# Low parts of the up-projection's weights: a subtraction on VectorE, or a negation on ScalarE and an accumulating DMA

## The chip, the cores and the metric

The kernel runs on one core of a Trainium2 chip. A core has TensorE (matmuls, in the profile PE, its weight loads PEld), VectorE (DVE), ScalarE (ACT), GpSimd (POOL) and SyncE (SP), which issues DMAs. Each engine takes its instructions in the order of its own list and waits at each for the semaphores that it names. The metric is device time in microseconds of one execution.

## What is computed

The reference is one step of a model with two layers of width 1024, over 512 prompt tokens and 8 sequences of 4 new tokens. The 544 tokens are handled together. Layer 0 mixes by gated linear attention (GLA), layer 1 by dilated attention; behind each stands a feed-forward stage. The change lies in that stage only:

```python
def _conv_ffn(h, w_up, conv_w, conv_b, w_down, buf):
    T = h.shape[1]
    u = h @ w_up                                   # 1024 -> 2 x 2816
    ux = jnp.concatenate([buf.astype(u.dtype), u], axis=1)
    c = conv_b + sum(ux[:, i:i + T] * conv_w[i] for i in range(CONV_WIDTH))
    gate, val = jnp.split(c, 2, axis=-1)
    return (jax.nn.silu(gate) * val) @ w_down, ux[:, -(CONV_WIDTH - 1):]
```

Everything is float32.

## The kernel before

Products of float32 accuracy are made of three matmuls. Weights and activations are each split into a high part, the value rounded to 12 bits by a cast to float32r, and a low part, the exact rest. `product` (line 95) multiplies high by high, high weights by low activations and low weights by high activations, for each of the 128-row pieces k of the contraction, into one PSUM tile per half of the tokens. For the up-projection there are 8 pieces and 2 halves (256 and 288 columns), so 48 matmuls in a product; for the down-projection 11 pieces, so 66.

`split_w` (line 85) makes the parts of a weight tile: ScalarE casts to `whi` (line 90), VectorE subtracts that from the raw weights to `wlo` (line 91). `whi` and `wlo` have two buffers each. Raw weights lie in two buffers of the tag `wraw` that all stages share, filled by `load_w` (line 80) through SyncE's queue, whose order is that of the program.

`ffn(l, ...)` runs once for each layer. Its 22 up tiles of 256 columns (128 of the gate, 128 of the value, so two products each) come in two halves of 11. Behind each half stand 8 products of the down-projection, with weights `wd` of 704 KB. A tile's product leaves PSUM on VectorE times 1/rms of the token (line 566), goes through the convolution (lines 576 to 578), silu (129) and the gating (583 to 585), and is split again (588, 589). The row of 1/rms (`rstd`) is worked out from the sums of squares `acc` where it is first asked for: two matmuls `pss` (line 180), two logarithms (181) and an exponential. The activations' parts `xh` and `xl` (157, 158) and the squares (166, 170) are made by `Normed.add` as the stage before finishes each x. In layer 0 the stage also works out tables for the attention: products `pbt` (619) and copies `sk` in DRAM, issued between the weights' loads.

The engines' lists are made when the program is built, by a scheduler that plays the program through on a timeline of its own. Loads on SyncE keep the program's order; the rest is put where that timeline has it ready first. So each place at which the order differs is looked up in the built programs.

Of the kernel before, what the change touches and what calls it, by code (L numbers as in the profile page):

```python
# [12 lines left out]
F32R = mybir.dt.float32r  # L13
# [6 lines left out]
P = 128  # L20
# [16 lines left out]
def trunk(ctx: ExitStack, tc: tile.TileContext, A, O, stage=4):  # L37
# [7 lines left out]
    def dma(out, in_):  # L45
        """Loads, in the order in which they are used."""
        tc.keep_in_program_order(nc.sync.dma_start(out, in_))
# [14 lines left out]
    # ---------------------------------------------------------------- background work  # L62
# [3 lines left out]
    def tick():  # L66
        """One stage of each lane's first generator, between the matmuls of a product."""
        for lane in reversed(lanes):
            if lane:
                try:  # L70
                    next(lane[0])
                except StopIteration:
                    lane.popleft()
# [5 lines left out]
    # ---------------------------------------------------------------- weights  # L79
# [5 lines left out]
    def split_w(raw, k0, k1, c0, m=P):  # L85
        """Two parts of a weight tile that add up to it exactly, each of 12 bits."""
# [10 lines left out]
    def product(w, xh, xl, ranges, done, m=P):  # L97
        """w.T x of float32 accuracy, in two halves of the tokens; done(half, psum) takes each."""
# [12 lines left out]
    # ---------------------------------------------------------------- constants  # L111
# [11 lines left out]
    def exp(out, in_, **kw):  # L123
        last_exp[0] = act(out, in_, AF.Exp, **kw)  # L124

    def silu(out, in_):
        """Behind every Exp so far, as the two sit in different sets of tables."""
# [4 lines left out]
    def log_exp():  # L132
        """The set of tables that holds both, loaded behind the last Silu and ahead of the block."""
# [10 lines left out]
    class Normed:  # L144
        """x * gain in two exact parts, tile by tile as x comes; the row of 1/rms, on every partition,
        is worked out where it is first asked for."""
# [5 lines left out]
        def add(self, k, x, spare=None):  # L152
            """A spare pool: GpSimd takes half of the squares, with a sum of its own."""
# [31 lines left out]
    def scaled(nx, out, scale=None, m=P):  # L185
        """What takes a product: times 1/rms, to SBUF."""
# [12 lines left out]
    # ---------------------------------------------------------------- GLA  # L199
    def gla(nxt):  # L200
# [24 lines left out]
        # the gates' second product: [hi | lo | hi] of the first against [hi | hi | lo] of the weights  # L225
# [21 lines left out]
        # zero outside of what the heads write  # L247
# [9 lines left out]
        def gates(h, G):  # L257
            # log-sigmoid of the gates, before the division
# [12 lines left out]
            # sums of the gates inside of a chunk  # L271
# [22 lines left out]
        def chain(h, q, k, v, G):  # L294
# [3 lines left out]
            # values, token-major  # L298
# [8 lines left out]
            # [hi | lo | hi] of the sample group's values and [hi | hi | lo] of its keys  # L307
# [7 lines left out]
            # decays over whole chunks: F[..., 0:2], [2:5], [5:9] bring keys to the end of chunk 1, 2, 3,  # L315
            # [9:13] queries to the start of the 128 tokens, 13 the state over all of them
# [16 lines left out]
            # the sample group's rows: 32 (b mod 4) + 4 (b // 4) + s  # L333
# [28 lines left out]
            # scores inside of the chunks  # L362
# [23 lines left out]
            # scores against the earlier chunks of the 128 tokens  # L386
# [49 lines left out]
            # sample group  # L436
# [47 lines left out]
        # the output's operands take the places of tiles that the heads are done with  # L484
# [47 lines left out]
    # ---------------------------------------------------------------- ConvFFN  # L532
    def ffn(l, x, nx, dst, tables=None, nxt=None):
        first = load_w(A["wu"][l, 0], KT, 256, "wu")
        with ExitStack() as es:
# [13 lines left out]
            half = NFF // 2  # L549
            for hf in range(2):  # L550
                gh, gl = [], []
                for ii in range(half):
                    next(bt, None)
                    i = hf * half + ii
                    raw = load_w(A["wu"][l, i], KT, 256, "wu") if i else first
                    cc = []
                    for s in range(2):
# [13 lines left out]
                        product(split_w(raw, 0, KT, s * P), nx.xh, nx.xl, BYTOK, done)  # L571
# [30 lines left out]
    # ---------------------------------------------------------------- dilated attention  # L602
    def bias_tables(bp, out):
        """Bias by distance for every group and head, skewed in DRAM so that a strided read gives the
        tile [query, head, key]; distances outside of the window hold NEG."""
        n = (383, 255, 63)
        # the row pitch as read, and the rows as written (number of runs, their pitch, a run's rows, their
        # pitch): each row so much further on as its queries are later
# [29 lines left out]
    def dilated(nx, xold, tables, nxt):  # L638
        first = load_w(A["wdi"][0], KT, 256, "wdi")
        with ExitStack() as es:  # L640
# [33 lines left out]
            # The prompt's tokens by their remainders of the group's dilation. The tiles of groups 1 and 2 take  # L674
            # every fourth token, and their queries lie by the remainder of 16 first.
# [42 lines left out]
            # ---- prompt  # L718
            # a unit: four tiles of 128 queries by 128 keys, or half of that many blocks by two; of a tile
            # its number, its first block of keys, its column and its width. Group 2's tiles are 4 by 32  # L720
            # queries of 4 by 32 keys, of which a query sees its own 32.
# [3 lines left out]
            def split_scores(q, k):  # L725
                """For each of two heads [hi; lo] of its queries, [hi; hi] of its keys, and the keys' lo: two
                products that add up to all but lo by lo."""
# [13 lines left out]
            def softmax(st, h, todo):  # L741
                """exp(scores + bias - max) of tiles of queries, with the max and the sum of it."""
# [586 lines left out]
```

## Time and profile before

| | |
|---|---|
| median of 3 runs | 1809.33 us (1807.87 to 1809.41) |
| the profiled execution, first to last instruction | 1809.7 us |
| TensorE busy | 1792.2 us (99%) |
| VectorE busy | 1091.2 us (60%) |
| ScalarE busy | 804.6 us (44%) |
| GpSimd busy | 224.4 us (12%) |
| DMA, mean over the span | 131 GB/s, 236.24 MB |

Layer 0's feed-forward stage runs from about 278 to 688 us, layer 1's from 1406 us to the end; GLA stands ahead of the first, dilated attention between the two. The profile holds, for one execution, each instruction with its engine, line, duration and what its engine waited for ahead of it. An idle engine matters only where the chain of waits that ends last passes through it.

### The profile page before, as it was taken

The numbers are of one execution on the slowest core, as the hardware profiler recorded it, in microseconds if no ns is written. First come the engines' busy times: TensorE is split into PE (matmuls) and PEld (weight loads), VectorE is DVE, ScalarE is ACT, GpSimd is POOL, SyncE is SP. The second block draws the span as 40 slices with busy tenths as digits, with TensorE's granted clock in tenths as the row PEclk, the third lists the DMA queues.
The fourth block names the chain that finished last, engine by engine and source line by source line (L and its number), as shares of the span: only waits on it lengthen the run. The fifth ranks groups of instructions, "written<-read, shape, count | busy, mean of one in ns | idle before, by whom it ended". The sixth has DMA issues, their size and how long they took to land.

```text
span 1809.7 us, 35651 instructions
## 1 busy us (share of the span) xinstructions
PE 1792.2 (99%) x14774; PEld 1683.1 (93%) x14774; DVE 1091.2 (60%) x2552; ACT 804.6 (44%) x1549; POOL 224.4 (12%) x416
## 2 busy tenths in 40 slices
PE   7999999999999999999999999999999999999999
PEld 7999999999999999988898888888887999999999
DVE  7565556764476645666575656565664667446652
ACT  5454534442244334644556365546452544224431
POOL 3000100110011010111012010201121011001110
PEclk9999999999999999999999999999999999999999
DMA  5033432432422344255436453544474222232232
GB/s 180 27 129 141 151 113 79 151 104 81 149 80 91 102 157 159 83 195 194 170 118 218 174 179 130 205 166 160 155 241 154 71 94 80 81 110 90 75 102 86
DMA packets 55266, 236.24 MB, mean 131 GB/s; under 512 B 11470, under 2 KB 20896, under 8 KB 37056
## 3 DMA queue, kind: packets, MB, share of 16 engines
q1 hardware_dynamic: 36816, 145.61, 23.3%
q0 software_dynamic: 18288, 88.36, 14.0%
q8 instruction: 116, 1.90, 0.4%
q14 instruction: 46, 0.38, 0.1%
HBM read 210.32 MB, written 29.33 MB: 132 GB/s over the span
## 4 chain that ended last, share of the span: by engine, by line
PE 98%; DMA 1%; DVE 1%; issue 0%; ACT 0%; SPq 0%; DVEq 0%; ACTq 0%
PE ps L104 82%; PE po L902 2%; PE pdo L1004 2%; PE pd L944 2%; PE ptr L887 1%; PE psc L795 1%; PE pn L694 1%; PE psc L794 1%; DMA vc<-in_dv 1%; PE pn L695 1%; PE px L391 1%; PE pvt L762 1%; PE psc L797 0%; PE pu L403 0%; PE po L418 0%
## 5 line engine op out<-in xcount | busy, mean ns | idle before, releaser
L104 PE MATMUL ps<-xh,whi 128*128 128x256 f32 (+2 forms) x3056 | 892.0, 293 | 7.1 <-ACT xh L157 5.5
L104 PE MATMUL ps<-xl,whi 128*128 128x256 f32 (+2 forms) x3056 | 886.5, 290 | 3.3 <-DVE xl L158 3.2
L104 PE MATMUL ps<-xh,wlo 128*128 128x256 f32 (+2 forms) x3056 | 886.9, 291 | 0.0
L104 PEld LDWEIGHTS ps<-xh,whi 128*128 128x128 f32 (+1 forms) x3056 | 577.2, 189 | 38.7 <-issue 29.6
L104 PEld LDWEIGHTS ps<-xh,wlo 128*128 128x128 f32 (+1 forms) x3056 | 576.9, 189 | 11.5 <-issue 9.5
L104 PEld LDWEIGHTS ps<-xl,whi 128*128 128x128 f32 (+1 forms) x3056 | 577.2, 189 | 11.1 <-DVE xl L158 5.5
L104 PE MATMUL ps<-gl,whi 128*128 128x272 f32 x704 | 198.8, 287 | 0.0
L104 PE MATMUL ps<-gh,whi 128*128 128x272 f32 x704 | 198.5, 288 | 0.3 <-DVE x L196 0.3
L104 PE MATMUL ps<-gh,wlo 128*128 128x272 f32 x704 | 195.8, 287 | 0.0
L566 DVE TENSOR_TENSOR u<-ps,rstd 128x256 f32<-128x256 f32 x176 | 74.4, 423 | 140.6 <-PE ps L104 140.2
L90 ACT CAST whi<-wu 128x1024 fp32r<-128x1024 f32 x88 | 92.7, 1053 | 97.2 <-PE ps L104 97.2
L104 PEld LDWEIGHTS ps<-gh,whi 128*128 128x128 f32 x704 | 132.2, 188 | 0.5 <-DVE x L196 0.5
L104 PEld LDWEIGHTS ps<-gl,whi 128*128 128x128 f32 x704 | 132.6, 188 | 0.0
L196 DVE TENSOR_TENSOR x<-ps,x 128x272 f32<-128x272 f32 x108 | 46.8, 440 | 141.4 <-PE ps L104 137.7
L104 PEld LDWEIGHTS ps<-gh,wlo 128*128 128x128 f32 x704 | 130.9, 188 | 0.0
L90 ACT CAST whi<-wd 128x768 fp32r<-128x768 f32 x64 | 50.2, 785 | 171.4 <-PE ps L104 142.0
L91 DVE TENSOR_TENSOR wlo<-wu,whi 128x1024 fp32r<-128x1024 f32 x88 | 107.5, 1222 | 30.7 <-ACT whi L90 30.7
L90 ACT CAST whi<-wdi 128x1024 fp32r<-128x1024 f32 x72 | 75.5, 1048 | 79.6 <-PE ps L104 71.1
L91 DVE TENSOR_TENSOR wlo<-wdi,whi 128x1024 fp32r<-128x1024 f32 x72 | 88.0, 1222 | 27.5 <-ACT whi L90 27.1
L572 POOL COPY uo<-u 128x18 f32<-128x18 f32 x88 | 52.3, 594 | 399.6 <-DVE u L568 399.6
L588 ACT CAST gh<-g 128x544 fp32r<-128x544 f32 x44 | 28.5, 648 | 132.6 <-DVE g L585 132.6
L124 ACT ACTIVATE ex<-ex,nm 128x128 f32<-128x128 f32 (+2 forms) x192 | 74.7, 393 | 19.4 <-DVE nm L748 19.1
(307 smaller groups left out, 2409.6 us busy)
## 6 DMA issues: line engine op xcount, KB each, us to landing
wu<-in_wu SPq DMA_DIRECT2D x44, 1024.0 KB, 4.9
wdi<-in_wdi SPq DMA_DIRECT2D x36, 1024.0 KB, 4.8
vc<-in_dv POOLq DMA_DIRECT2D x28, 1024.0 KB, 6.0
wd<-in_wd SPq DMA_DIRECT2D x32, 704.0 KB, 4.2
kc<-in_dkA POOLq DMA_DIRECT2D x16, 1024.0 KB, 5.3
kc<-in_dkB POOLq DMA_DIRECT2D x16, 768.0 KB, 4.8
out_vo<-v POOLq DMA_DIRECT2D x24, 256.0 KB, 3.1
out_ko<-k POOLq DMA_DIRECT2D x24, 256.0 KB, 3.2
```

The lines of the kernel that those rows point to most:

```text
L90: nc.scalar.copy(hi, r)
L91: tt(out=lo, in0=r, in1=hi.bitcast(F32), op=ALU.subtract)
L104: mm(ps[:m, :b - a], ww, xx[k][:, a:b], start=(k == 0 and s == 0), stop=(k == kt - 1 and s == 2))
L124: last_exp[0] = act(out, in_, AF.Exp, **kw)
L196: tt(out=out[:, c], in0=ps, in1=old[:, c], op=ALU.add)
L391: mm(ps[:32 * c, t, 32 * c - 32:32 * c], keys, qh[:, t * P + 32 * c:t * P + 32 * c + 32], start=True, stop=True)
L566: tt(out=u[:, 2 + c0:258 + c0], in0=ps[:, :256], in1=nx.rstd[:, c0:c0 + 256], op=ALU.mult)
L572: nc.gpsimd.tensor_copy(out=uo[:, f, :].rearrange("p (b t) -> p b t", t=2), in_=u[:, 512:566].rearrange("p (b t) -> p b t", t=6)[:, :, :2])
L588: nc.scalar.copy(h_, g)
L902: mm(o, R[g][2][:, kb, r], PT[n - 2][:, h, c:c + P], start=(n == 2 and i == 0), stop=(n - 1 == len(units)), skip_group_check=True)
L944: mm(pd[32 * qd:32 * qd + 32, a0:a1], qz[g][:, qd // 2, qd % 2, 32 * b:32 * b + 32], kc[4 * part + b][:, qd, a0:a1], start=False, stop=(b ...
L1004: mm(po[32 * qd:32 * qd + 32, :], PT[:, t, 32 * qd:32 * qd + 32], vc[t][:, qd, :], start=False, stop=(t == 6), skip_group_check=True)
```

## The change

In `ffn` the up-projection's weights are no longer split by `split_w`. A new function `prepare` loads a raw tile, has ScalarE write its negative, rounded to float32r, for all 256 columns into a new tile `ulo`, and has GpSimd issue a DMA that reads the same weights from DRAM once more and adds them to `ulo`. What is left there is weights minus rounded weights. `parts` makes the high part on ScalarE as before, a product at a time. `prepare` is called one tile ahead, and the stage's first load stands behind those of `cw` and `cs`, no longer ahead of them. The down-projection still uses `split_w`.

```diff
     def ffn(l, x, nx, dst, tables=None, nxt=None):
-        first = load_w(A["wu"][l, 0], KT, 256, "wu")
         with ExitStack() as es:
...
             half = NFF // 2
+
+            def prepare(i):
+                raw = load_w(A["wu"][l, i], KT, 256, "wu")
+                lo = ft.tile([P, KT, 256], F32R, name="ulo", bufs=3)
+                nc.scalar.activation(lo, raw, AF.Copy, scale=-1.0)
+                nc.gpsimd.dma_start(lo.rearrange("p k n -> p (k n)"), A["wu"][l, i], accum_op=ALU.add)
+                return raw, lo
+
+            def parts(raw, lo, c0):
+                hi = wp.tile([P, KT, P], F32R, name="whi", tag="whi")
+                nc.scalar.copy(hi, raw[:, :, c0:c0 + P])
+                return [(hi[:, k, :], lo[:, k, c0:c0 + P]) for k in range(KT)]
+
+            ready = [prepare(0)]
             for hf in range(2):
                 gh, gl = [], []
                 for ii in range(half):
                     next(bt, None)
                     i = hf * half + ii
-                    raw = load_w(A["wu"][l, i], KT, 256, "wu") if i else first
+                    raw, lo = ready.pop()
+                    if i + 1 < NFF:
+                        ready.append(prepare(i + 1))
...
-                        product(split_w(raw, 0, KT, s * P), nx.xh, nx.xl, BYTOK, done)
+                        product(parts(raw, lo, s * P), nx.xh, nx.xl, BYTOK, done)
```

`ulo` has three buffers, in the stage's own pool. That pool takes the memory of the stage ahead: in layer 0 the first `ulo` lies over a tile `ogh` that GLA's output projection reads to its end. In the changed program lines behind the new functions have higher numbers: the negation is line 555, the accumulating DMA 556, the cast of `parts` 561.

The built programs differ at three places. The first is ScalarE's list where layer 0's feed-forward stage begins. `xh` and `sq` belong to the last x of the stage ahead. Before:

```order
L157 ACTIVATE xh_3097<-x,gains 128x544
L166 ACTIVATE sq<-x 128x544
L90 CAST whi<-wu 128x1024
L157 ACTIVATE xh_3162<-x,gains 128x544
L166 ACTIVATE sq<-x 128x544
L181 ACTIVATE rstd<-pss,eps 128x272
L90 CAST whi<-wu 128x1024
L181 ACTIVATE rstd<-pss,eps 128x272
L124 ACTIVATE rstd<-rstd 128x544
```

And the same place in the changed program:

```order
L166 ACTIVATE sq<-x 128x544
L181 ACTIVATE rstd<-pss,eps 128x272 x2
L555 ACTIVATE ulo<-wu 128x2048
L561 CAST whi<-wu 128x1024
L124 ACTIVATE rstd<-rstd 128x544
L561 CAST whi<-wu 128x1024
```

The two casts of the first up tile stood among the last norms; now the negation stands behind both logarithms, and the casts behind it. In layer 1 the negation stands behind the last `sq`, the two casts follow it, and the logarithms follow them.

The second is TensorE's list at the same place, from the last matmul of GLA's output projection. Before, the first up product follows at once, and `pss` comes 52 rows later:

```order
L104 MATMUL ps<-ogh,wlo 128x272
L104 MATMUL ps<-xh_2702,whi 128x256
L104 MATMUL ps<-xl_2703,whi 128x256
L104 MATMUL ps<-xh_2702,wlo 128x256
L104 MATMUL ps<-xh_2766,whi 128x256
```

In the changed program:

```order
L104 MATMUL ps<-ogh,wlo 128x272
L180 MATMUL pss<-acc,ones 128x272 x2
L636 MATMUL pbt<-oh_3198,rb 16x383
L636 MATMUL pbt<-oh_3199,rb 16x255
L636 MATMUL pbt<-oh_3200,rb 16x63
L104 MATMUL ps<-xh_2702,whi 128x256
L104 MATMUL ps<-xl_2703,whi 128x256
L104 MATMUL ps<-xh_2702,whi 128x288
L104 MATMUL ps<-xl_2703,whi 128x288
L104 MATMUL ps<-xh_2702,whi 128x256
L104 MATMUL ps<-xl_2703,whi 128x256
L104 MATMUL ps<-xh_2702,ulo 128x256
```

`pss` and `pbt` moved ahead of all up matmuls, and six matmuls with high parts stand ahead of the first that reads `ulo`. In layer 1 `pss` stands ahead of the up matmuls too.

The third is the turn from the first down half to the second up half, here ScalarE's list in layer 0. Before:

```order
L90 CAST whi<-wd 128x768
L90 CAST whi<-wd 128x640
L90 CAST whi<-wu 128x1024 x3
L576 ACTIVATE c_5442<-u_3187,cw 128x560
```

And in the changed program:

```order
L90 CAST whi<-wd 128x768
L90 CAST whi<-wd 128x640
L555 ACTIVATE ulo<-wu 128x2048
L561 CAST whi<-wu 128x1024 x3
L593 ACTIVATE c_5437<-u_3185,cw 128x560
```

The casts of the twelfth up tile stand behind the negation of the thirteenth. On SyncE's list 12 loads of `wu` stand ahead of the first 8 loads of `wd`, not 11. The twelfth tile keeps one buffer of `wraw` until its casts, behind that down half; in the built program all eight of those loads go to the other buffer, where before they took turns.

## The prediction

> **What bounds the kernel now.** I read the page's busy times first, then the chain of waits, then both halves of the first feed-forward stage by windows.
>
> ```profile
> span 1809.7 us, 35651 instructions
> PE 1792.2 (99%) x14774; PEld 1683.1 (93%) x14774; DVE 1091.2 (60%) x2552; ACT 804.6 (44%) x1549; POOL 224.4 (12%) x416
> ```
>
> TensorE is busy for all but 17.5 us. The chain of waits from 410 to 500 us is a single piece, the matmuls of line 104, and the windows say the same of the up half (277.56 to 421) and of the down half (421 to 488). In a window's row the columns are the length, then busy us and instructions of PE, PEld, DVE, ACT and POOL, then the granted clock, the DMA engines' busy share and GB/s.
>
> ```profile
> 409.93 90.10 PE ps L104 x720
> 277.56:421.00 143.44, 143.44 (x1136) 142.34 (x1135) 96.15 (x171) 61.60 (x78) 22.32 (x44) 1.00 0.33 108
> 421.00:488.00 67.00, 67.00 (x539) 66.83 (x538) 23.84 (x38) 13.97 (x17) 0.20 (x1) 1.00 0.37 127
> ```
>
> One matmul takes 90.10 / 720 = 0.125 us. So one up tile (2 products of 48 matmuls) takes 12.0 us, half of a tile 6.0 and one product of the down half (66) 8.25. TensorE has no idle time in either half. Whatever VectorE is spared there is worth nothing; the change can only add waits, or leave the time as it is.
>
> **What is removed and added in the steady run.** Groups of instructions, with busy us and mean ns, and the DMA table, with KB and us to landing:
>
> ```profile
> L91 DVE TENSOR_TENSOR wlo<-wu,whi 128x1024 fp32r<-128x1024 f32 x88 | 107.5, 1222 | 30.7 <-ACT whi L90 30.7
> L90 ACT CAST whi<-wu 128x1024 fp32r<-128x1024 f32 x88 | 92.7, 1053 | 97.2 <-PE ps L104 97.2
> L90 ACT CAST whi<-wd 128x768 fp32r<-128x768 f32 x32 | 26.8, 839 | 132.7 <-PE ps L104 109.5 <-issue 22.4 <-ACT acc L166 0.8
> L157 ACT ACTIVATE xh<-x,gains 128x544 fp32r<-128x544 f32 x32 | 23.0, 744 | 1.8 <-PE ps L104 0.9 <-DMA x<-in_xT 0.5 <-DVE x L196 0.3
> L588 ACT CAST gh<-g 128x544 fp32r<-128x544 f32 x44 | 28.5, 648 | 132.6 <-DVE g L585 132.6
> wu<-in_wu SPq DMA_DIRECT2D x44, 1024.0 KB, 4.9
> vc<-in_dv POOLq DMA_DIRECT2D x28, 1024.0 KB, 6.0
> wd<-in_wd SPq DMA_DIRECT2D x32, 704.0 KB, 4.2
> ```
>
> VectorE loses 88 subtractions, 107.5 us, all of it beside matmuls: 0. ScalarE gains 44 negations of 2048 columns. From 768 to 1024 columns a cast grows by 214 ns, so 2048 columns take 1.05 + 4 x 0.214 = 1.91 us, and a form with a scale takes 0.10 more (744 against 648): 2.0 us, 88 us in all. Beside 12.0 us of matmuls per tile this is hidden too. GpSimd issues 44 DMAs that carry another 46 MB. It has nothing queued there but copies of 18 columns, so its queue costs nothing.
>
> The trace has no accumulating DMA. Call its time from issue to landing X. The nearest row is a plain load of the same size from GpSimd's queue, 6.0 us, which is the lower bound: the same bytes must move. A store of 8 KB shows the part that doesn't scale:
>
> ```profile
> scr<-st POOLq DMA_DIRECT2D x8, 8.0 KB, 2.3
> ```
>
> So 3.7 us of the 6.0 is moving. An accumulation reads its destination as well as its source, so I take the moving part twice, X = 2.3 + 2 x 3.7 = 9.7 us. Three passes, 13.4, are the upper end. Nothing suggests less than a plain load.
>
> The Trainium skill ("Collectives: The Full Stack", on the fold count and why AG, RS and AR differ) says that an add inside the DMA costs through its second source read, not through the add, and gives 62.28 against 32.35 GB/s. By that ratio X would be 9.4 and the whole sum 0.6 us less; no run here shows it yet.
>
> In the steady run a negation stands ahead of the next tile's cast on ScalarE. The load that it waits for goes out when the tile before last has been cast (1.05 us into a tile), lands 4.9 later, the negation takes 2.0 and the cast 1.05: 9.0 us, where the cast is needed at 12.0. That leaves 3.0 us. The accumulation then has about 16 us until its low parts are used. With X = 9.7 I put this at 0.
>
> **The first start, near 278 us.** Here the change moves instructions. The rows show the end of the output projection as it runs now:
>
> ```profile
> 255.87 0.33 SPq L47 DMA_DIRECT2D wu<-in_wu  x1
> 277.56 0.28 PE L104 MATMUL ps<-xh,whi 128*128 128x256 f32 x1
> 277.63 1.05 ACT L90 CAST whi<-wu 128x1024 fp32r<-128x1024 f32 x1 [3.78 <-PE ps L104]
> 277.76 0.44 DVE L196 TENSOR_TENSOR x<-ps,x 128x272 f32<-128x272 f32 x1 [2.16 <-PE ps L104]
> 279.24 0.64 ACT L166 ACTIVATE sq<-x 128x544 f32<-128x544 f32 x1
> 279.86 0.78 DVE L158 SCALAR_TENSOR_TENSOR xl<-x,gains,xh 128x544 fp32r<-128x544 f32 x1
> 280.56 0.72 DVE L170 TENSOR_TENSOR acc<-acc,sq 128x544 f32<-128x544 f32 x1
> 284.71 0.49 ACT L181 ACTIVATE rstd<-pss,eps 128x272 f32<-128x272 f32 x1 [4.82 <-PE pss L180]
> ```
>
> From the chain of waits, pss and the products of the tables (pbt), which run between the up matmuls now:
>
> ```profile
> 284.21 0.92 PE pss L180 x4
> ...
> 287.51 1.28 PE pbt L619 x6
> ```
>
> Now the first up product starts at 277.56, the moment the projection ends, and the sum of squares (pss) is slipped in 6.6 us later. In the changed order pss stands ahead of every up matmul, and the first negation stands on ScalarE behind both logarithms of pss. Step by step: the last x is complete at 277.76 + 0.44 = 278.2; xh takes 0.74 to 278.9; xl 0.78 and acc 0.72 follow on VectorE, to 280.4; pss starts there, its first logarithm 0.5 later, and with two of 0.49 ScalarE is free at 282.0. The negation ends at 284.0. Only then can GpSimd issue the accumulation, which lands at 284.0 + X. Meanwhile TensorE can do pss (0.92), pbt (1.28) and the 6 high-part matmuls that stand ahead of the first low one (0.75), 2.95 us. The stage's first load, moved behind those of cw and cs on SyncE, goes out at 255.87 now and isn't wanted before 282.0: 0. The start is late by 284.0 + 9.7 - 277.56 - 2.95 = **13.2 us**.
>
> **The second start, near 1406 us.**
>
> ```profile
> 1403.82 3.32 ACT L157 ACTIVATE xh<-x,gains 128x544 fp32r<-128x544 f32 x5 [0.90 <-PE ps L104]
> 1406.25 0.42 PE L104 MATMUL ps<-xh,whi 128*128 128x256 f32 x2
> 1407.98 1.39 ACT L157 ACTIVATE xh<-x,gains 128x544 fp32r<-128x544 f32 x2
> 1409.28 0.65 ACT L166 ACTIVATE sq<-x 128x544 f32<-128x544 f32 x1
> 1417.76 0.40 PE L104 MATMUL ps<-xh,whi 128*128 128x288 f32 x1 [1.61 <-DVE u L566]
> ```
>
> ScalarE makes seven xh from 1403.82 (3.32 + 1.39) and the last square (0.65), to 1409.1; here the negation follows at once, to 1411.1. Up matmuls start at 1406.25 now. Done meanwhile are pss and 6 matmuls, 1.67 us, and the wait of 1.61 us at 1417.76 goes, as its rstd will be long there. Late by 1411.1 + 9.7 - 1406.25 - 1.67 - 1.61 = **11.3 us**.
>
> **The clock.** Both starts leave TensorE idle for most of 13 us. What the clock does then is seen at the program's start only:
>
> ```profile
> 6.30:10.30 4.00, 3.96 (x16) 1.00 1.05 363
> 14.20:17.10 2.90, 2.59 (x10) 0.54 0.97 358
> 24.00:28.00 4.00, 4.00 (x34) 1.00 0.89 326
> ```
>
> After idling, 16 matmuls took the time of 34; and 14.20 to 17.10 was slow again, at a clock of 0.54. Each costs about 4.00 x (1 - 16/34) = 2.1 us or, in the shorter stretch, 2.59 - 10 x 4.00 / 34 = 1.4. I take 2.0 for each start, **4.0 us**.
>
> The Trainium skill ("TensorE: Matmul & The Clock Gate", Part 1, What's actually happening) states half rate after an idle window of about 3.4 us and full rate after as long a busy one. By it the two starts would cost 1.7 us each, 3.4; the rows above agree on half rate.
>
> **The turn between the halves.** A tile's load now goes out one tile ahead, so the twelfth up tile holds one of the two places for raw weights through the first down half, and its eight loads share the other.
>
> ```profile
> 427.23 0.84 ACT L90 CAST whi<-wd 128x768 fp32r<-128x768 f32 x1 [5.59 <-PE ps L104]
> 429.08 0.73 ACT L90 CAST whi<-wd 128x640 fp32r<-128x640 f32 x1 [1.01 <-DVE wlo L91]
> 429.85 0.83 DVE L91 TENSOR_TENSOR wlo<-wd,whi 128x640 fp32r<-128x640 f32 x1 [0.20 <-ACT whi L90]
> 435.45 0.84 ACT L90 CAST whi<-wd 128x768 fp32r<-128x768 f32 x1 [5.64 <-PE ps L104]
> 455.74 0.57 SPq L47 DMA_DIRECT2D sk<-vd  x1
> ```
>
> A place is free at 429.85 + 0.83 = 430.7, the next load lands 4.2 later at 434.9, and its cast is due at 435.45: 0.5 us to spare, 0 cost; without that cover each us is paid up to seven times in each stage. After the eighth product's weights the order puts the negation of tile 13 ahead of the casts of tile 12. In the same clock: free 430.7, load 435.6, negation 437.6, cast 438.65, while the product runs out at 429.08 + 8.25 = 437.3: 1.4 us late. In the first stage a copy of a table (sk) is issued ahead of that load, 0.57, and moves beside it; I take 2.4 there. Together **3.8 us**.
>
> **Sum.** 13.2 + 11.3 + 4.0 + 3.8 = 32.3 us on the profiled execution's 1809.7: 1842.0. The median of the runs, 1809.33, stands 0.4 below that span, so 1842 serves for both. With X = 6.0, 1.4 us for each clock dip and nothing at the turns it is 19.9 more (1829.6); with X = 13.4 and twice the turns 43.5 more (1853).
>
> **Rivals.**
> (a) The accumulation is a matter of throughput: a tile's takes longer than the 12.0 us of its matmuls, and both up halves run at the queue's pace. At 15 us this adds 44 x 3.0 = 132 us, to 1974; it decides from 12.0 us on. For it: three passes would be 13.4 with the fixed part. Against: plain loads share the engines with a busy share of 0.33 in the up half. Chance 0.12.
> (b) The plain load slowed by the accumulation beside it. The 3.0 us on ScalarE are used up when a load takes over 7.9 us. At twice 4.9, some 32 of the 44 tiles wait 1.9 us, 61 in all, 1903; at 1 us each, 1874. For it: with X = 9.7 the accumulation, issued about 8 us into a tile, runs into the next tile's load. Against: it overlaps only for some 5 us. Chance 0.15.
> (c) Not slower: matmuls of the up half get faster once VectorE no longer reads and writes weights beside them. There are 4224; to be faster in the end each must lose (32.3 + 3.6) / 4224 = 8.5 ns of its 125. For it: VectorE is busy 67% there. Against: in the down half, at 36%, a matmul takes the same (67.00 / 539 = 0.124). Chance 0.03.
> (d) The starts overlap better than I have it, slower by 4 to 19 us: 0.04.
>
> **How the numbers follow.** The forecast's own case (1829 to 1853) has 0.66. The range takes in it and the milder part of (b): 1829 to 1885. A measurement can tell about 0.2%, 3.6 us, from no change. Faster is (c) alone, 0.02; within 0.2% are its weaker form and an edge of (d), 0.02; slower 0.96.
>
> **What would show it.** In the changed profile: TensorE waits for the DMA of ulo once in each stage, some 8 us, at about 286 and in the second stage, with a dip of the clock behind; a wait for whi of one to three us behind each first down half; L555 at 2.0 us; no wait in between. X is read from the DMA table. I am wrong if ulo lands over 13 us after its issue, if line 104 waits at every tile, or if the first up matmuls run on without the wait.

## The result, and the profile after

The changed kernel takes 1908.28 us (median of 4 runs, 1905.21 to 1911.46), the kernel before 1809.37 beside it: ratio 1.0544, 95% interval 1.0531 to 1.0556. It is slower by 98.9 us, three times the 32.3 forecast, and above the range. In two experiments one run took about twice as long (3471.65 us in no_second_read, 4236.22 in negate_behind_cast) and is left out; in the second it was the profiled one, so negate_behind_cast has a time but no profile.

From the page of the kernel after, in the same columns as before; the last two rows are from the table of DMA issues.

```profile
span 1909.7 us, 35685 instructions
PE 1818.8 (95%) x14774; PEld 1700.9 (89%) x14774; DVE 996.0 (52%) x2464; ACT 873.7 (46%) x1593; POOL 228.8 (12%) x460
...
L555 ACT ACTIVATE ulo<-wu 128x2048 fp32r<-128x2048 f32 x44 | 84.2, 1914 | 139.6 <-DMA wu<-in_wu 134.9
...
wu<-in_wu SPq DMA_DIRECT2D x44, 1024.0 KB, 6.8
ulo<-in_wu POOLq DMA_DIRECT2D x44, 1024.0 KB, 8.7
```

The prices of the new operations were forecast well: the negation is 1.91 us (2.0 forecast), the accumulation lands in 8.7 (9.7 forecast). What was not forecast is in the row above it: the plain load of the same tile, 4.9 us before, now takes 6.8. And TensorE, with the same 14774 matmuls, is idle for 90.9 us, not 17.5, and busy for 1818.8, not 1792.2.

Where this lies is read from windows by stage. First before: first up half, first down half and second up half of layer 0, then of layer 1 (length, then busy us of PE, PEld, DVE, ACT and POOL, the granted clock, the DMA share, GB/s).

```profile
277.56:412.52 134.96, 134.96 (x1069) 133.86 (x1068) 90.44 (x161) 58.44 (x73) 21.47 (x42) 1.00 0.33 110
412.52:478.33 65.81, 65.81 (x531) 65.81 (x530) 24.20 (x38) 14.27 (x18) 0.85 (x2) 1.00 0.36 123
478.33:611.10 132.77, 132.77 (x1059) 132.60 (x1058) 89.53 (x160) 54.83 (x65) 20.61 (x39) 1.00 0.26 87
...
1406.25:1541.55 135.30, 133.69 (x1062) 133.33 (x1061) 93.04 (x165) 59.17 (x73) 21.05 (x42) 1.00 0.24 82
1541.55:1607.47 65.92, 65.92 (x530) 65.92 (x529) 24.23 (x38) 14.29 (x18) 0.86 (x2) 1.00 0.29 99
1607.47:1740.21 132.74, 132.74 (x1059) 132.60 (x1057) 89.60 (x160) 53.80 (x64) 20.91 (x39) 1.00 0.24 83
```

The same of after; the first up half has two rows in each layer, the start up to the landing of the first `ulo`, and the rest:

```profile
276.48:292.94 16.46, 6.53 (x16) 3.18 (x16) 1.86 (x3) 9.03 (x12) 1.79 (x2) 0.59 0.46 106
292.94:446.10 153.16, 139.12 (x1051) 137.28 (x1052) 63.87 (x134) 69.05 (x73) 20.94 (x51) 0.95 0.67 170
446.10:518.07 71.97, 68.67 (x530) 67.32 (x528) 25.72 (x42) 16.73 (x22) 1.74 (x4) 0.98 0.30 100
518.07:668.86 150.79, 137.80 (x1056) 136.64 (x1057) 65.98 (x137) 68.87 (x74) 20.30 (x49) 0.97 0.59 150
...
1462.43:1478.61 16.18, 3.23 (x13) 2.42 (x11) 4.29 (x7) 9.59 (x12) 1.76 (x2) 0.65 0.58 136
1478.61:1624.13 145.52, 135.84 (x1051) 134.40 (x1052) 64.63 (x135) 69.40 (x73) 20.85 (x51) 0.98 0.61 149
1624.13:1692.62 68.49, 66.64 (x530) 65.97 (x528) 25.21 (x41) 16.46 (x21) 1.74 (x4) 1.00 0.27 90
1692.62:1840.15 147.53, 137.03 (x1056) 136.32 (x1057) 66.19 (x137) 67.84 (x73) 20.21 (x49) 0.97 0.58 146
```

By the forecast's own bookkeeping the first start is late by 292.94 - 277.56 - 2.95 = 12.4 us and the second by 16.18 - 1.67 - 1.61 = 12.9. Behind the starts the up halves are 21.1, 18.0, 13.5 and 14.8 us longer than before (before's first halves without the 2.95, and the 1.67 and 1.61, that were counted at the starts). These four make 67.4 us. In them TensorE idles for 14.0 + 13.0 + 9.7 + 10.5 = 47.2; the other 20.2 are the same matmuls at a lower clock. The first down halves add 6.2 and 2.6. With 1.5 us that the rest became shorter, that is the 100.0 us between the two spans.

TensorE's waits name the place:

```profile
PE ps L104 <- ACT whi L561: 50.2, 24, 4.9
PE ps L104 <- DMA ulo<-in_wu: 14.7, 2, 8.7
```

The second row is the start, once in each stage as forecast. Of the 24 waits for the cast of high parts in the first row, two small ones belong to the first start (0.86 and 0.22 us) and two to the turns (1.04 and 1.00). The other twenty, 47.1 us, stand in the up halves, where the forecast has none. The chain of waits shows how they come about, in layer 0's first up half, then in its second, then in layer 1:

```profile
361.41 8.82 DMA wu<-in_wu
...
370.34 0.04 ACT ulo L555
...
372.15 1.03 ACT whi L561
373.18 0.77 ACT c L593
...
373.97 0.81 DVE c L594
...
376.22 1.04 ACT whi L561
...
377.27 8.90 DMA wu<-in_wu
...
531.99 10.35 DMA wu<-in_wu
...
618.91 6.90 DMA wu<-in_wu
...
1560.13 6.96 DMA wu<-in_wu
...
1574.15 6.79 DMA wu<-in_wu
```

In none of the three stretches (361.41 to 377.27, 531.99 to 618.91, 1560.13 to 1574.15) is there a matmul. It is a closed loop of ScalarE and the load: the second cast of a tile (376.22) frees a place for raw weights, the next load goes out at once (377.27), the negation waits for it at the head of ScalarE's list, behind the negation stands the first cast of the next tile, behind that the convolution's `c` and the silu, and behind these the second cast, which frees the next place. VectorE is a member too: ahead of the silu ScalarE waits 1.71 us for VectorE's two steps of `c`. From load to load it is 377.27 - 361.41 = 15.9 us in layer 0 and 1574.15 - 1560.13 = 14.0 in layer 1, where a tile's matmuls take 12.0. Without the load, 7.0 and 7.1 us of it are left: the loop's period is some 7.05 us plus the landing of `wu`. The second up halves run in the same loop. At most of their tiles the first cast stands ahead of the negation and drops out of it, which leaves 6.1 us beside the load; but the loads take longer there (8.1 us in the median in layer 0), and the six periods from 531.99 to 618.91 are 14.5 us on average.

The lower clock is seen behind a wait of 3.59 us for `whi` and not behind one of 2.05. First the two waits, from TensorE's timeline, then a window behind each; the last columns are clock, DMA share and GB/s:

```profile
373.23 0.58 PE L104 MATMUL ps<-xh,whi 128*128 128x256 f32 x1 [3.59 <-ACT whi L561]
...
420.95 0.39 PE L104 MATMUL ps<-xh,whi 128*128 128x256 f32 x1 [2.05 <-ACT whi L561]
```

```profile
374.50:376.50 2.00, 2.00 (x11) 2.00 (x11) 1.50 (x4) 0.86 (x2) 0.40 (x2) 0.50 0.57 122
...
422.00:424.00 2.00, 2.00 (x19) 2.00 (x18) 1.73 (x4) 0.64 (x2) 0.38 (x2) 1.00 0.73 131
```

Eleven matmuls in 2 us against nineteen: such a wait is paid a second time in part. By the Trainium skill ("TensorE: Matmul & The Clock Gate", Part 1, What's actually happening) the half rate follows an idle window of about 3.4 us; these two waits lie on either side of that and agree. So do the others in the up halves: all six of 3.59 to 4.92 us are followed by a lower clock, and none of 2.13 us or less. One wait elsewhere does not agree: it is 1.76 us long, ends at 457.00 in layer 0's first down half, and the granted clock of the 2 us behind it is 0.50 as well. So the length alone does not decide; what does stays open.

### The profile page after: what moved, and what is told of

Same layout as the page of the kernel before. It is cut to its first block, busy times and chain, and to the rows that moved or that the text cites. A ratio compares the mean times of both kernels' runs of the same rounds, so it can differ in the third digit from the quotient of the medians.

```text
span 1909.7 us, 35685 instructions
## 1 busy us (share of the span) xinstructions
PE 1818.8 (95%) x14774; PEld 1700.9 (89%) x14774; DVE 996.0 (52%) x2464; ACT 873.7 (46%) x1593; POOL 228.8 (12%) x460
## 4 chain that ended last, share of the span: by engine, by line
PE 69%; DMA 15%; issue 8%; ACT 5%; DVE 3%; ACTq 0%; SPq 0%; POOL 0%; POOLq 0%; DVEq 0%
PE ps L104 54%; DMA wu<-in_wu 12%; ACT whi L561 3%; PE po L919 2%; PE pdo L1021 2%; PE pd L961 1%; DMA wd<-in_wd 1%; DVE c L594 1%; ACT c L593 1%; PE ptr L904 1%; DMA ulo<-in_wu 1%; PE psc L812 1%; PE pn L711 1%; PE psc L811 1%; PE pn L712 1%
## 5 line engine op out<-in xcount | busy, mean ns | idle before, releaser
L104 PE MATMUL ps<-xl,whi 128*128 128x256 f32 (+2 forms) x3056 | 896.5, 293 | 4.1 <-DVE xl L158 4.0
L104 PEld LDWEIGHTS ps<-xh,whi 128*128 128x128 f32 (+1 forms) x3056 | 585.7, 192 | 93.2 <-ACT whi L561 56.5
L104 PEld LDWEIGHTS ps<-xl,whi 128*128 128x128 f32 (+1 forms) x3056 | 585.8, 192 | 11.9 <-DVE xl L158 6.3
L104 PE MATMUL ps<-xh,wlo 128*128 128x272 f32 (+3 forms) x1648 | 481.4, 293 | 0.0
L104 PE MATMUL ps<-xh,ulo 128*128 128x256 f32 (+1 forms) x1408 | 412.5, 293 | 14.7 <-DMA ulo<-in_wu 14.7
L104 PEld LDWEIGHTS ps<-xh,wlo 128*128 128x128 f32 (+1 forms) x1648 | 312.1, 189 | 11.1 <-issue 9.5
L104 PEld LDWEIGHTS ps<-xh,ulo 128*128 128x128 f32 x1408 | 272.4, 194 | 15.3 <-DMA ulo<-in_wu 15.3
L594 DVE SCALAR_TENSOR_TENSOR c<-u,cw,c 128x560 f32<-128x560 f32 x88 | 70.5, 802 | 221.4 <-ACT c L593 221.3
L555 ACT ACTIVATE ulo<-wu 128x2048 fp32r<-128x2048 f32 x44 | 84.2, 1914 | 139.6 <-DMA wu<-in_wu 134.9
L561 ACT CAST whi<-wu 128x1024 fp32r<-128x1024 f32 x88 | 90.9, 1036 | 24.7 <-PE ps L104 24.6
```

Source lines behind the costliest of these rows:

```text
L104: mm(ps[:m, :b - a], ww, xx[k][:, a:b], start=(k == 0 and s == 0), stop=(k == kt - 1 and s == 2))
L555: nc.scalar.activation(lo, raw, AF.Copy, scale=-1.0)
L561: nc.scalar.copy(hi, raw[:, :, c0:c0 + P])
L594: stt(c, u[:, 1:561], cw[:, f, 1:2], c, ALU.mult, ALU.add)
```

## The experiments

Theory L is that loop, closed because the accumulation slows the load beside it. The rivals are ScalarE's order without the slow load (S), throughput (A), and contention of the traffic itself (C).

**Is it the second read, and is it the read or the add?** Two kernels: no_second_read has the first line of this edit alone, plain_second_read both.

```diff
-                nc.gpsimd.dma_start(lo.rearrange("p k n -> p (k n)"), A["wu"][l, i], accum_op=ALU.add)
+                nc.gpsimd.dma_start(lo.rearrange("p k n -> p (k n)"), A["wu"][l, i])
```

> Leaves out the accumulating DMA, so the low parts are only the negated weights; everything else of the changed kernel stays. Theory L (loop): in the changed kernel an up tile's pace is a closed loop over the two places for raw weights: load, negation 1.87 us, first cast 1.03, the stretch with c 3.04, second cast 1.04, next load; the 8.8 us load makes it 15.9 where the matmuls take 12.0, and the load is long because the accumulation moves beside it. Without it the load takes 4.9 again, the loop 11.9, and TensorE waits less than 0.2 us per tile. What stays is about 5 and 3 us at the two starts (the negation still stands ahead of the first cast) and 2 to 4 at the turns: 1817 to 1825 us. Rival S (ScalarE's order alone, the load having little part): the waits for whi in the up halves stay above 2 us per tile, and the time is 1880 to 1895.

> The second read of the weights stays, with the same bytes from the same queue, but as a plain load without the add, so the low parts are the weights themselves. It tells which half of theory L's load is to blame. L-traffic (any second read beside the load slows it): wu still takes 7.5 to 9 us to land and the time is 1885 to 1910. L-add (it is the add that holds the DMA engines): ulo lands in about 6 us, wu in 5 to 6, the loop is 12 to 13 us, and the time is 1825 to 1860, of which 2 x 6 to 8 us are the starts.

The low parts are then the negated weights alone, or the weights themselves. Measured: 1823.45 us without it (ratio 1.0067, 1.0050 to 1.0084) and 1832.55 with the plain read (1.0115, 1.0098 to 1.0132). TensorE's waits for `whi` in no_second_read (us in total, times, longest):

```profile
PE ps L104 <- ACT whi L560: 3.0, 3, 1.2
```

The DMA table of plain_second_read (the row for `wu` reads the same in no_second_read):

```profile
wu<-in_wu SPq DMA_DIRECT2D x44, 1024.0 KB, 4.9
ulo<-in_wu POOLq DMA_DIRECT2D x44, 1024.0 KB, 5.3
```

From the timelines of GpSimd and SyncE in plain_second_read, layer 1:

```profile
1476.51 0.53 POOL L556 DMA_DIRECT2D ulo<-in_wu  x1 [1.49 <-ACT ulo L555]
...
1481.25 0.33 SPq L47 DMA_DIRECT2D wu<-in_wu  x1
```

S falls: with the same negation at the same place on ScalarE and a load of 4.9 us, the loop is 7.05 + 4.9 = 11.95 us, just inside 12.0, and the waits in the up halves are gone. L-traffic falls too, for this kernel: the same bytes as a plain load land in 5.3 us and leave the load at 4.9, and TensorE waits for `whi` 6.5 us in all. But the plain read also lies beside the load for less time. The next load goes out 4.74 us behind its issue, when it is all but over; in the changed kernel the distance is the same (1569.41 and 1574.15), and the accumulation of 8.7 us then runs on for some 4 us. So it is the add, by the time for which it keeps the transfer going; what a plain read beside the load for as long would do to it is not shown. 85 of the 98.9 us hang on this one DMA, 76 on its being an accumulation, the waits at the starts included.

**Opening the loop.** Three places for raw up weights in one kernel; in the other two places, but the negation behind the second cast on ScalarE and not ahead of the first.

```diff
-                raw = load_w(A["wu"][l, i], KT, 256, "wu")
+                if i % 3 == 2:
+                    raw = ft.tile([P, KT, 256], F32, name="wu3", bufs=1)
+                    dma(raw.rearrange("p k n -> p (k n)"), A["wu"][l, i])
+                else:
+                    raw = load_w(A["wu"][l, i], KT, 256, "wu")
```

That is three_raw. In negate_behind_cast `prepare` only loads (but for tile 0), and a new function `low` holds its negation and its accumulation:

```diff
-                        product(parts(raw, lo, s * P), nx.xh, nx.xl, BYTOK, done)
+                        w = parts(raw, lo, s * P)
+                        if s and ready:
+                            with tc.issue_after(last_cast[0].ins):
+                                ready[0] = (ready[0][0], low(i + 1, ready[0][0]))
+                        product(w, nx.xh, nx.xl, BYTOK, done)
```

> Every third tile of raw up weights gets a place of its own, so there are three places in place of two; nothing else changes. Theory L: the load goes out a tile (12 us) earlier, the loop has 24 us or more of matmuls to hide in, and the waits for whi in the up halves vanish though wu still takes 7 to 9 us to land. The starts stay (12.4 and 12.9 us late, about 2 each for the clock): 1836 to 1846 us. Rival A (throughput: a tile's load and accumulation together take more DMA time than 12 us of matmuls give): a third place only moves the wait, and the time stays within 1895 to 1912.

> Two places as in the changed kernel, but the negation of the next tile and its accumulation stand on ScalarE behind the second cast of the present tile, not ahead of the first one. Theory L: the load no longer has to be there for a cast, so its loop is gone; the accumulation now goes out some 3.3 us into a tile and lands 8.7 later, at 12.0, where the first low part is needed at 12.25. So TensorE waits for ulo 0 to 1.5 us per tile instead of for whi 3.9: 1838 to 1885 us with the starts as they are. Rival A: the pace stays at 14 to 16 us per tile, the wait merely moves from whi to ulo, 1895 to 1912.

Measured: 1858.71 us (1.0263, 1.0248 to 1.0279) and 1867.41 (1.0305, 1.0285 to 1.0326). A falls: throughput would have held both at 1895 or above. The second is within L's range; for it the time alone speaks, but behind_and_first below has the same order with a profile, and there TensorE waits for `whi` once, for 0.60 us. In three_raw both second up halves are back at 132.2 and 132.3 us though `wu` takes 6.4 and `ulo` 9.0, and the first up half of layer 1 is longer than before by its start alone (14.4). But 1858.71 misses L's 1836 to 1846. What is too much lies in layer 0's first up half (163.4 us from 277.56). TensorE waits there for VectorE's `u`, which stands behind `c` of ScalarE, which stands behind a negation that waits for its load; two loads on that chain, at 357.27 and 387.45, take 19.93 and 22.22 us to land. From the timeline of SyncE (start, us):

```profile
371.21 6.68 SPq L47 DMA_DIRECT2D wu<-in_wu  x1
377.94 0.61 SPq L47 DMA_DIRECT2D sk<-vd  x1
```

SyncE needs 6.68 us to issue one load, 0.33 elsewhere. Three loads are held up so (4.53, 6.68 and 6.61 us), all in the stretch in which it also issues the copies of tables (`sk`).

**The starts alone.** Tile 0 of each stage is split by VectorE, all else is as changed.

```diff
                 raw = load_w(A["wu"][l, i], KT, 256, "wu")
+                if i == 0:
+                    return raw, None
...
             def parts(raw, lo, c0):
+                if lo is None:
+                    return split_w(raw, 0, KT, c0)
```

> The changed kernel, but tile 0 of each stage is split by VectorE as before, so no accumulation stands ahead of a stage's first low part; all other tiles as changed. Theory L with the starts as forecast: the two starts (12.4 and 12.9 us late in the changed profile, about 1.5 each for the clock) are gone and the loop stays: 1908 - 28 = 1880, 1874 to 1887 us. Rival H (the starts are slack that the loop would take anyway, since its first load has a head start): less than half of it comes back, 1893 to 1908 us.

Measured: 1892.59 us (1.0463, 1.0429 to 1.0496): 16 of the 28 came back. The time is 0.4 us below H's range, less than the runs differ (1889.30 to 1902.65), but more than half came back. The row for `ulo` is gone from TensorE's waits, and that for `whi` is as it was:

```profile
PE ps L104 <- ACT whi L565: 51.9, 25, 5.1
```

In layer 0 the first up matmul is still late (285.91 against 277.56), since `pss` still stands ahead of it and the casts behind its logarithms, and the loop, to whose first loads a long start gives a lead, makes its first wait for `whi` at 325 us in place of 344. So 12.4 and 12.9 were the right sizes of what was seen, but not of what its removal is worth.

**The traffic with nobody waiting for it.** The kernel before, plus the negation and accumulation of each tile into tiles that nothing reads. In the first version the scheduler put the negation a tile early, ahead of a cast; in the second it is held behind its tile's second cast.

```diff
                         product(split_w(raw, 0, KT, s * P), nx.xh, nx.xl, BYTOK, done)
+                        if s:
+                            lo = ft.tile([P, KT, 256], F32R, name="ulo", bufs=3)
+                            with tc.issue_after(last_cast[0].ins):
+                                nc.scalar.activation(lo, raw, AF.Copy, scale=-1.0)
+                            nc.gpsimd.dma_start(lo.rearrange("p k n -> p (k n)"), A["wu"][l, i], accum_op=ALU.add)
```

The line with `issue_after` is in before_unused_late alone.

> The kernel before, with VectorE's subtraction as it was, plus the negation and the accumulating DMA of every tile behind its second cast, into tiles that nothing reads. It measures the accumulation's traffic without anyone waiting for it. Theory L: wu takes 6 to 9 us to land here too, but its load has about 21 us until a cast needs it, so the time stays within 1809 to 1817 us. Rival C (the traffic, the 88 us on ScalarE or the copies cost time in themselves, by contention at SBUF or in the matmuls): 1825 to 1870 us, with matmuls over 0.127 us each or new waits for whi.

> Again the kernel before with the negation and the accumulation of every tile added and read by nobody, but the negation is held behind the second cast of its own tile on ScalarE (in before_unused it had been ordered a tile earlier, where it waited for the load in front of a cast). So the accumulation moves, and nothing waits for it or behind it. Theory L: the traffic alone costs little: 1809 to 1820 us, no wait for whi above 1 us in the up halves, though single loads of wu may take 8 us. Rival C (contention in itself): the time stays near that of before_unused, 1860 to 1880 us.

Measured: 1875.52 us (1.0362, 1.0344 to 1.0381) and 1826.03 (1.0087, 1.0070 to 1.0104). The first missed L's numbers, because the scheduler's order made it another experiment: its chain of waits passes through the same loop, with the subtraction behind the second cast as one more member. Unlike in the changed kernel, single products stand in this chain too.

```profile
353.56 11.11 DMA wu<-in_wu
...
370.75 1.24 DVE wlo L91
```

The two together show that 49 us are the place of one instruction per tile in ScalarE's list, at equal work and traffic. The second came out 6 us above L's range. Layer 1's stage (1421.77 to 1823.73) and layer 0's second up half are as before to 2 us; the rest is in layer 0's first up half:

```profile
278.20:429.94 151.74, 140.81 (x1082) 138.76 (x1081) 92.56 (x161) 75.89 (x84) 24.13 (x53) 0.96 0.71 173
495.75:628.49 132.74, 132.74 (x1059) 132.57 (x1057) 92.91 (x160) 72.47 (x76) 21.43 (x50) 1.00 0.75 173
1421.77:1823.73 401.96, 400.00 (x3174) 399.13 (x3172) 236.62 (x399) 176.01 (x194) 50.68 (x114) 1.00 0.58 145
```

The timeline of SyncE there:

```profile
357.71 12.17 SPq L47 DMA_DIRECT2D wu<-in_wu  x1
```

So C falls for the accumulation alone (the middle row: 132.74 us, as before to 0.03, at 173 GB/s against 87), and holds where copies of tables and accumulations move together, by loads that are held up.

**Both cures, and what is left.** behind_and_first joins negate_behind_cast and first_by_vector. behind_first_lowlast also puts the matmuls with low parts last in a tile's first product. early_first also moves the stage's first load ahead of the pools again. early_first_copies_down also issues the table copies beside the down products.

The edits of the last three, in this order, the first in `product` behind the loop of the high parts, the second ahead of the pools of `ffn`, the others in its up and down loops:

```diff
+            for k, (hi, lo) in enumerate(w if last else ()):
+                mm(ps[:m, :b - a], lo, xh[k][:, a:b], start=False, stop=(k == kt - 1))
...
+        first = load_w(A["wu"][l, 0], KT, 256, "wu")
...
-                    next(bt, None)
+                    if not hf and ii < 6:
+                        next(bt, None)
...
                 for m in range(KT):
+                    next(bt, None)
                     raw = load_w(A["wd"][l, hf, m], half, P, "wd")
```

> Both cures at once: the negation behind the second cast, and tile 0 of each stage by VectorE. Theory L: the order alone gave 1867, the starts are worth 28: 1839, 1832 to 1846 us, and what is left is TensorE waiting for ulo at each tile by up to 1 us (issue some 3.3 us into a tile, 8.5 to 9 to landing, needed at 12.25). Rival R: what is left in that order is not the accumulation's landing but something else (the load, ScalarE): then line 104 waits for whi, not for ulo.

> As behind_and_first, and in a tile's first product the 8 matmuls with low parts come last, behind the 16 with high parts, in each half of the tokens; so the first low part is needed 16 matmuls into the tile and not 2, 1.75 us later. Theory L: the waits for ulo at each tile go too: 1812 to 1824 us, level with the kernel before or up to 0.7% slower. Rival R: no better than behind_and_first, 1832 to 1846.

> As behind_first_lowlast (1837.5), and a stage's first load stands ahead of the pools again as in the kernel before, by which the first up matmuls of the first stage stand ahead of the sum of squares again. Theory: part of both starts is not the accumulation but this order; 5.6 us come back at the first start and 0 to 4 at the second: 1828 to 1833 us. Rival: the order costs nothing, 1836 to 1839.

> As early_first, and the twelve copies of the tables (sk) are issued beside the down products, not beside the up tiles of the first stage. Theory L: the waits for ulo that are left (11 us, all in the first stage beside these copies) go: 1816 to 1823 us. Rival M (they only move: the loads of wd take longer and TensorE waits for their casts): no gain over early_first, 1828 to 1834 us.

Measured: 1847.09 us (1.0207, 1.0185 to 1.0229), 1837.51 (1.0147, 1.0127 to 1.0167), 1830.00 (1.0107, 1.0086 to 1.0128) and 1828.22 (1.0097, 1.0082 to 1.0112). The first is 1 us above its range, and what TensorE waits for is `ulo`, as L said:

```profile
PE ps L106 <- DMA ulo<-in_wu: 16.7, 11, 3.7
```

The second missed its range by 13.5 us: `ulo` is waited for in 8 places still (11.6 us), all in layer 0, six of them between 351 and 425 us beside the table copies. The third met its range. In the fourth the waits for `ulo` are down to one of 1.5 us, but the copies now stand beside `wd` and the first down half takes 75.09 us, not 65.81: rival M, the cost moved. Layer 1, which has no such copies, is the clean case. Its whole stage in early_first_copies_down:

```profile
1423.02:1823.22 400.20, 398.61 (x3174) 397.61 (x3172) 190.10 (x357) 177.61 (x193) 50.27 (x113) 1.00 0.54 143
```

and the same stage of the kernel before:

```profile
1406.25:1806.29 400.04, 398.43 (x3174) 397.71 (x3172) 230.38 (x399) 140.50 (x172) 47.36 (x92) 1.00 0.26 88
```

With tile 0 on VectorE and loaded early, the negation behind the cast and low parts last, the change costs nothing there and gains nothing: 40.3 us less work on VectorE, 37.1 more on ScalarE, twice the DMA share, the same time. No version came out ahead of the kernel before.

**The copies in the changed kernel.** Only the table copies moved, by the last edit above, in the kernel as changed.

> The changed kernel as it is, but the twelve copies of the tables (sk) are issued beside the down products of the first stage and not beside its up tiles. Theory L: a tile's period in a first up half is 6.98 us plus the landing of wu; without the copies the loads there land in 6.8 to 7.1 us as in the second stage, not 8.8, and the period is 13.8 to 14.1, not 15.9; six to eight tiles times 1.9, 11 to 15 us with the clock behind the waits, come back, and 5 to 12 are lost again in the first down half, where the copies now stand beside wd: 1897 to 1908 us. Rival K (the copies have no part in the 8.8 us; the first stage differs in something else): the period stays at 15.9 and the time at 1908 or above.

Measured: 1908.00 us (1.0531, 1.0502 to 1.0559), on the edge between the two ranges; the period decides. From its chain of waits in the first up half:

```profile
351.52 7.39 DMA wu<-in_wu
...
365.97 6.64 DMA wu<-in_wu
...
379.65 7.12 DMA wu<-in_wu
...
393.82 7.60 DMA wu<-in_wu
```

The three periods from 351.52 to 393.82 are 14.1 us on average, the three loads 7.05: again 7.05 between them, and layer 0 now runs like layer 1. K falls. The up half became shorter by 3.8 us (157.6 from its first matmul, against 161.5) and the down half longer by 2.6, so it bought nothing. That is less than expected: only four periods of the changed kernel had been at 15.9 us.

## Why the prediction was wrong, point by point

- **The steady run: the step that failed.** "That leaves 3.0 us ... I put this at 0." The 67.4 us are 47.2 of waiting and 20.2 of clock; 4.1 of the clock belong to the starts (see below), so this step cost 63.3. The other terms held better: the starts 25.3 for 24.5, their clock 4.1 for 4.0, the turns with the first down halves 8.8 for 3.8. Two things were wrong in it. The 9.0 us of the working (1.05 + 4.9 + 2.0 + 1.05) left out what stands on ScalarE between a tile's first and second cast, `c`, the wait for VectorE's part of it and the silu, 376.22 - 372.15 - 1.03 = 3.0 us; with them there was no slack at all (7.05 + 4.9 = 11.95 of 12.0). And the load did not stay at 4.9: it landed in 6.8 us in the median beside the accumulation, and in up to 10.35. Undoing one of the two is enough: with the load at 4.9 the loop fits (no_second_read), and with a third place a load of 6.9 in the median is hidden (layer 0's second up half of three_raw).
- **Rival (b)** was the mechanism. That its price for a load of twice 4.9, 1903, is near the result is luck: most loads were shorter than that, a load of 8.9 us would by its reckoning wait 1.0 us, which it prices at 1874, and the clock behind the waits is not in it. I gave it 0.15 because accumulation and load would overlap "only for some 5 us"; that was so (some 4 us), but with no slack each of these microseconds counts. It also took the loop to start losing at 7.9 us, where it does at about 4.95.
- **X** was 8.7 us in the median, 9.7 forecast, inside 6.0 to 13.4. The lower bound was not the nearest row: the profile before also has `kc`, 1024 KB from the same queue in 5.3 us, just what the plain second read took. Taking off the 2.3 us that do not scale, the accumulation moves for 6.4 us and the plain second read for 3.0, 2.1 times as long. That agrees with the ratio of 1.93 in the Trainium skill ("Collectives: The Full Stack", The bandwidth ceiling: the fold count and why AG ≠ RS ≠ AR), given there for collectives. What I did not draw from it is that a transfer that holds the engines twice as long also holds up the load beside it.
- **The starts**, 13.2 and 11.3 forecast, were 12.4 and 12.9: right, with the mechanism named. Undoing them gave only 16 us, since the loop takes up part of it.
- **The clock**, 4.0 for the dips behind two starts: at 0.125 us a matmul, 52 matmuls in the 8.06 us from 292.94 and 39 in the 7.39 from 1478.60 are 1.6 and 2.5 us too slow, 4.1 together, so the size was right. These are part of the 20.2 us; the rest stands behind waits that were not forecast. Of the rows that the forecast was read from, the first has a granted clock of 1.00, so only its count of matmuls and the second row speak for a lower clock.
- **The turn**, 3.8 forecast: the waits for the casts of tile 12 are there but shorter (1.04 and 1.00 us). They lie within the 6.2 and 2.6 us that the first down halves lost, so 6.7 us of these fall on the down products, put at 0. In layer 0 the cover of 0.5 us was used up: the wait of 1.76 us at 457.00 is for a cast behind a load of `wd` that took 5.41 us, not 4.2, and the lower clock follows it.
- **VectorE's 107.5 us**, put at 0: right. Rival (c) did not happen: with the subtractions gone and nothing waiting, layer 1's stage takes 400.20 us, with them 400.04.
- **Rival (a)** did not happen: a tile's load and accumulation fit into 12 us as soon as nothing waits for the load.

## What to carry to other kernels

When an instruction that waits for a load is put ahead of other work on an in-order engine, follow the load's place back: who frees it, and does that stand behind the new instruction? If so there is a loop, and its period is the sum of all its members, those of other lists included; only then ask what the load's own duration becomes beside the new transfers. Work taken from an engine that bounds nothing is worth nothing, so such a change can only be bought at exactly zero.

## What the runs showed of the hardware

An accumulating transfer fills the DMA engines at a low rate. Windows in layer 1 of the changed kernel (clock, DMA share and GB/s last), the accumulation alone and then beside the load that goes out at 1574.15:

```profile
1570.50:1574.10 3.60, 3.60 (x32) 3.60 (x32) 2.04 (x4) 1.89 (x4) 0.40 (x2) 1.00 0.93 157
1574.15:1575.50 1.35, 1.35 (x12) 1.35 (x11) 0.59 (x1) 0.73 (x1) 0.00 (x0) 1.00 1.03 218
```

The same load alone, in the kernel before:

```profile
1648.00:1650.00 2.00, 2.00 (x18) 2.00 (x17) 0.80 (x2) 0.71 (x2) 0.65 (x1) 1.00 0.98 410
```

A share of 0.93 at 157 GB/s against 0.98 at 410: I read this as engines with nothing to spare for a load next to it, which then takes 7 us where it took 4.9. Nor had I expected that SyncE's issue of one load grows from 0.33 to 6.7 (three_raw) and 12.2 us (before_unused_late) in a stretch where copies of the tables in DRAM, accumulations and loads meet. Their meeting alone is not enough: in the changed kernel, where all three meet too, no load's issue takes over 0.36 us. What held it up was not tried and stays open.
